# Rows of the stream's split blocks 32 bytes longer: each block at another byte modulo 256

## The chip, the cores and the metric

The kernel runs on one core of one Trainium2 chip. The metric is the device time of one execution in microseconds, as the median of the runs of a kernel. One further execution was taken with the hardware profiler; all rows below come from it.

## What is computed

A decoder trunk of two layers over 512 tokens of width 1024, all in float32. Each layer is two half-weighted SwiGLU blocks around a mixer: an mLSTM in the first layer, a sparse attention with shared keys and values (computed once, between the layers) in the second. Cut to what matters here:

```python
def swiglu(h, w_in, w_out):                      # w_in (1024, 5632), w_out (2816, 1024)
    a, b = jnp.split(h @ w_in, 2, axis=-1)
    return (jax.nn.silu(a) * b) @ w_out

for layer in range(2):
    h = h + 0.5 * swiglu(rmsnorm(h, ffn_norm[layer, 0]), ffn_w_in[layer, 0], ffn_w_out[layer, 0])
    hn = rmsnorm(h, mix_norm[layer])
    h = h + (mlstm_mixer(hn, ...) if layer == 0 else nsa_mixer(hn, kv, ...))
    h = h + 0.5 * swiglu(rmsnorm(h, ffn_norm[layer, 1]), ffn_w_in[layer, 1], ffn_w_out[layer, 1])
    if layer == 0:
        kv = nsa_shared_kv(h, ...)
```

## The kernel before

The stream is kept transposed, as eight blocks `h[b]` of 128 features by 512 tokens. Every product is made of split operands: an operand is written as a high part (rounded to the matmul's input type, `float32r`) and a low part (what is left), and `mm3` (line 145) adds three matmuls, high by high, high weight by low stream, low weight by high stream. In the trace a matmul's name is out<-moving,stationary, so the three are `pmm<-xhi,whi`, `pmm<-xlo,whi` and `pmm<-xhi,wlo`. Each has its own weight load of 128x128 (the rows of PEld), then streams the 512 columns of the moving block.

The weights come in by DMA, 512 KB at a time, into `wraw`; ScalarE and VectorE split them into `whi` and `wlo` (lines 124 and 125), two weights ahead of their use. The stream's blocks are split once per stage by `norm_in`: `parts(b)` scales block b by the norm's gain and writes `xhi` on ScalarE (line 187) and `xlo` on VectorE (line 188). All eight pairs stay for the whole stage. The pool `x` has eight buffers of each of the two tags, so block b of every stage is in buffer b. In the mixers the same buffers serve a second time, as `yhi`/`ylo` (line 559) and `ohi`/`olo` (line 947), the split inputs of the output projections, made by `split` (lines 152 and 153).

The stages follow each other: `ffn0`, `mlstm`, `ffn1`, `kv`, `ffn2`, `nsa`, `ffn3`. A `ffn` stage (line 256) goes in three parts of 8, 7 and 7 pairs of strips: for each pair, 2x8 `mm3` against the eight x blocks (line 289), then `gate` on VectorE and ScalarE gives `ghi`/`glo`, and eight output blocks of 7 or 8 `mm3` each against these (line 307). That is 22 pairs x 16 x 3 = 1056 matmuls on x blocks and 528 on g blocks in each of the four. The blocks go in the order k = 0 to 7 for one strip, then for the other (the first pair of a part goes strip by strip within k). In the mixers x blocks are the moving operand of the projections, or, in `project_v` and for the values of `kv`, the stationary one against moving weights.

How the buffers lie: pools are placed one after the other, and a buffer's start is rounded up to 32 bytes. In the program as built, the h blocks, `wraw`, `whi`, `wlo`, `xhi` and `xlo` all begin at 128 modulo 256 in each partition (the first `xhi` at byte 69248, then every 2048 bytes). A strip of 128 weights is 512 bytes, so every strip begins at 128 modulo 256 too. In the `ffn` stages a tile `home` of 384 bytes (line 262) stands ahead of the others, and `ghi` and `glo` begin at 128 modulo 256 as well. In `mlstm` the stage's own tiles begin at 192 modulo 256, in `nsa` the large ones at 0 or at 64. In `compress` of the `kv` stage the stationary operand is a slice `Fh[:, m, :]` of 124 columns, 496 bytes, so its start moves back by 16 bytes modulo 256 with each m.

The order of the instructions on each engine is that in which the code issues them; nothing in it depends on addresses.

Of the kernel before, what the change touches and what calls it, by code (L numbers as in the profile page):

```python
# [11 lines left out]
F32R = mybir.dt.float32r  # L12
# [7 lines left out]
P = 128  # L20
T = 512
# [69 lines left out]
class Net:  # L91
# [83 lines left out]
    def norm_in(self, gcol, ssq=True, loaded=False):  # L175


        nc = self.nc
        x, acc = [], []
        if ssq:  # L180
            acc = [self.sp.tile([P, T], F32, name=f"ssq{i}", tag=f"ssq{i}") for i in range(2)]

        def parts(b):
            hi = self.xp.tile([P, T], F32R, name="xhi", tag="xhi")
            lo = self.xp.tile([P, T], F32R, name="xlo", tag="xlo")
            g = self.g[:, gcol + b:gcol + b + 1]
            nc.scalar.activation(hi, self.h[b], AF.Copy, scale=g)
            nc.vector.scalar_tensor_tensor(lo, self.h[b], g, hi.bitcast(F32), op0=ALU.mult, op1=ALU.subtract)
            x.append((hi, lo))

        def squares(b):
            t = acc[b // 4]
            if b % 4 == 0:
                nc.scalar.activation(t, self.h[b], AF.Square)
            else:
                sq = self.sp.tile([P, T], F32, name="sq", tag="sq", bufs=2)
                nc.scalar.activation(sq, self.h[b], AF.Square)  # L197
                (nc.gpsimd if b < 4 else nc.vector).tensor_tensor(t, t, sq, op=ALU.add)  # L198

        for b in range(KB):  # L200
            parts(b)
            if ssq and not loaded:
                squares(b)
        if ssq and loaded:
            for b in range(KB):
                squares(b)
        if ssq:
            nc.vector.tensor_tensor(acc[1], acc[1], acc[0], op=ALU.add)
        return x, acc[-1] if acc else None
# [102 lines left out]
    def mlstm(self):  # L312
        nc, tc = self.nc, self.tc
        TT, STT, TS = nc.vector.tensor_tensor, nc.vector.scalar_tensor_tensor, nc.vector.tensor_scalar
        with ExitStack() as ctx:
# [16 lines left out]
            def pair(name, src):  # L332

                t = mp.tile([P, T], F32R, name=name, tag="rows", bufs=2)
                nc.gpsimd.memset(t.bitcast(F32), 0.0)
                nc.scalar.activation(t[:H], src, AF.Copy)
                TT(t[32:32 + H], src, t[:H].bitcast(F32), op=ALU.subtract)
                return t
# [193 lines left out]
            def finish(half):  # L532

                d = dm[half]
                s = mp.tile([40, T], F32, name="ds", tag="tmp", bufs=3)
                nc.scalar.copy(s, d[:40])
                pt = ps_nm()[:, :160].rearrange("p (t c) -> p t c", t=NTB)
                for tb in range(NTB):
                    nc.tensor.transpose(pt[:, tb, :], s[:, tb * P:(tb + 1) * P], self.ident[:40, :40])
                dc = mp.tile([P, NTB, H], F32, name="dc", tag="dc", bufs=2)  # L540
                cf = mp.tile([P, NTB, H], F32, name="cf", tag="cf", bufs=2)
                nc.scalar.activation(dc, pt[:, :, :H], AF.Square)
                TT(dc, dc, e2, op=ALU.max)
                TS(dc, dc, EPS, None, op0=ALU.mult)
                STT(dc, pt[:, :, 32:], 1.0 / P, dc, op0=ALU.mult, op1=ALU.add)
                fl = lambda t: t.rearrange("p t h -> p (t h)")
                self.rsqrt(mp, fl(cf), fl(dc), "crt")
                pr = ps_nm()
                for tb in range(NTB):
                    nc.tensor.transpose(pr[:H, tb * P:(tb + 1) * P], cf[:, tb, :], self.ident)  # L550
                cr = pair("cr", pr[:H])
                yield
                for h in range(4 * half, 4 * half + 4):
                    pc = ps_nm()
                    self.mm(pc, pick(h), cr, True, True)
                    n = num[h]
                    STT(n, n, self.g[:, G_HEAD + h:G_HEAD + h + 1], pc, op0=ALU.mult, op1=ALU.mult)
                    (nc.vector if half else nc.gpsimd).tensor_tensor(n, n, sig[h], op=ALU.mult)
                    hi = self.xp.tile([P, T], F32R, name="yhi", tag="xhi")
                    lo = self.xp.tile([P, T], F32R, name="ylo", tag="xlo")  # L560
                    self.split(n, hi, lo)
                    y[h] = (hi, lo)
                    yield
# [33 lines left out]
            run(rest)  # L597
            sigmoids(0)
            weave(project_v(1), finish(0), 0.25)
            rest = chain(project_og(1), project_out(0))  # L600
            weave(heads(1), rest, 1.0)
            sigmoids(1)
            weave(finish(1), rest, 5)
            run(rest)
            run(project_out(1))
# [165 lines left out]
    def nsa(self):  # L771
        nc, tc = self.nc, self.tc
        TT, STT, TS = nc.vector.tensor_tensor, nc.vector.scalar_tensor_tensor, nc.vector.tensor_scalar
        with ExitStack() as ctx:
# [169 lines left out]

            def project_out(half):
                for k in range(4 * half, 4 * half + 4):
                    hi = self.xp.tile([P, T], F32R, name="ohi", tag="xhi")
                    lo = self.xp.tile([P, T], F32R, name="olo", tag="xlo")
                    self.split(o[k], hi, lo)
                    y[k] = (hi, lo)  # L950
                for m2 in range(4):
                    w = self.weight("n_out", half, m2)
                    for j in range(2):
                        ps = ps_mm()
                        for k in range(4):
                            self.mm3(ps, self.strip(w, 4 * j + k), y[4 * half + k], k == 0, k == 3)
                            yield
                        hh = self.h[2 * m2 + j]
                        TT(hh, ps, hh, op=ALU.add)
# [13 lines left out]
            def all_fronts():  # L973
                for h in range(QH):
# [16 lines left out]
                    fronted[0] = h + 1  # L991

            q0, backs, out0 = project_q(0), {}, project_out(0)

            read, started, fronted, qdone = [0, 0], [0], [0], [1]
# [24 lines left out]
            while fill.step():  # L1020
                pass
            assert fill.may is None
            run(project_out(1))

    def store(self):
# [121 lines left out]
```

## Time and profile before

| | us |
|---|---|
| median of 2 runs | 2048.72 (2048.69 to 2048.75) |
| the profiled execution | 2048.92 |
| its span, first to last instruction | 2047.1 |
| PE (matmuls) busy | 2026.3, 99% of the span |
| DVE busy | 1116.5, 55% |
| ACT busy | 816.5, 40% |

What lies around the span is 1.8 us. Matmuls are pipelined: one begins while the one before it still drains, so the busy time of one (389 ns) is longer than the step from its start to the next one's start. In a stream without waits the step is what the time is made of. The duration shown is the step plus a tail of some 162 ns that overlaps the next matmul, so that a nanosecond more in the duration is a nanosecond more in the step.

### The profile page before, as it was taken

Reading aid. Unit: us, or ns where it says so; the run is one execution under the profiler, and the core shown is the slowest. Engines: PE = TensorE matmul, PEld = TensorE weight load, DVE = VectorE, ACT = ScalarE, POOL = GpSimd, SP = SyncE. Lnnn points to the kernel's source line nnn. Section 1 sums busy time; section 2 is a strip of 40 time slices with the busy share of each in tenths; the row PEclk is TensorE's granted clock in tenths of the full one; section 3 lists DMA queues with packets and bytes.
Section 4 is the critical chain, followed back from the end, with each engine's and each line's share of the span. In section 5 each row is a group of like instructions: output and inputs, shape, how many; then the busy total and the mean of one; then the engine's idle time right before and its main releaser. Section 6 shows DMA issues by size and latency. Waiting matters only on the chain.

```text
span 2047.1 us, 24445 instructions
## 1 busy us (share of the span) xinstructions
PE 2026.3 (99%) x9468; PEld 1658.9 (81%) x9468; DVE 1116.5 (55%) x1814; ACT 816.5 (40%) x1410; POOL 166.8 (8%) x216
## 2 busy tenths in 40 slices
PE   8999999999999999999999999999999999999999
PEld 6888888788878888888888888888777788888887
DVE  6434445767865434445666444445778874434343
ACT  5313223445743222234343322224889863222231
POOL 1000000012200000000101000001444310000000
PEclk9999999999999999999999999999999999999999
DMA  4232332323123332333333323323111112332323
GB/s 161 94 101 94 94 103 86 113 80 95 64 73 103 93 102 87 102 96 97 103 106 121 117 93 91 105 88 103 51 42 47 37 62 93 94 102 88 105 94 95
DMA packets 56468, 188.12 MB, mean 92 GB/s; under 512 B 6816, under 2 KB 7456, under 8 KB 56352
## 3 DMA queue, kind: packets, MB, share of 16 engines
q1 hardware_dynamic: 55392, 184.47, 28.5%
q8 instruction: 74, 1.21, 0.2%
q0 software_dynamic: 384, 1.05, 0.2%
q10 hardware_dynamic: 576, 1.05, 0.1%
q14 instruction: 42, 0.34, 0.1%
HBM read 177.10 MB, written 2.10 MB: 88 GB/s over the span
## 4 chain that ended last, share of the span: by engine, by line
PE 91%; ACT 4%; DVE 3%; issue 1%; DMA 0%; POOL 0%; SPq 0%; ACTq 0%; DVEq 0%
PE pmm L143 81%; PE S L143 2%; PE po L143 2%; PE vps L143 1%; ACT pr L889 1%; PE pt L921 1%; PE paux L143 1%; DVE wlo L125 1%; PE pn L143 1%; ACT whi L124 1%; ACT pth L152 0%; PE dm L143 0%; PE pt L143 0%; ACT nx L886 0%; DMA wraw<-in_ffn_in 0%
## 5 line engine op out<-in xcount | busy, mean ns | idle before, releaser
L124 ACT ACTIVATE whi<-wraw 128x1024 fp32r<-128x1024 f32 (+3 forms) x399 | 360.3, 916 | 993.8 <-PE pmm L143 825.7
L143 PE MATMUL pmm<-xhi,whi 128*128 128x512 f32 x1672 | 657.9, 393 | 7.7 <-ACT whi L124 7.7
L143 PE MATMUL pmm<-xhi,wlo 128*128 128x512 f32 x1672 | 654.0, 391 | 0.3 <-DVE wlo L125 0.2
L143 PE MATMUL pmm<-xlo,whi 128*128 128x512 f32 x1672 | 653.1, 391 | 0.0
L125 DVE TENSOR_TENSOR wlo<-wraw,whi 128x1024 fp32r<-128x1024 f32 (+3 forms) x399 | 421.5, 1066 | 85.2 <-ACT whi L124 74.4
L143 PEld LDWEIGHTS pmm<-xhi,whi 128*128 128x128 f32 x1672 | 314.4, 188 | 71.0 <-ACT whi L124 9.2
L143 PEld LDWEIGHTS pmm<-xhi,wlo 128*128 128x128 f32 x1672 | 314.0, 188 | 67.9 <-DVE wlo L125 2.0
L143 PEld LDWEIGHTS pmm<-xlo,whi 128*128 128x128 f32 x1672 | 314.4, 188 | 61.8
L143 PE MATMUL pmm<-ghi,whi 128*128 128x512 f32 x704 | 274.1, 389 | 0.0
L143 PE MATMUL pmm<-ghi,wlo 128*128 128x512 f32 x704 | 273.9, 389 | 0.0
L143 PE MATMUL pmm<-glo,whi 128*128 128x512 f32 x704 | 273.9, 389 | 0.0
L271 DVE TENSOR_TENSOR fu<-pmm,r 128x512 f32<-128x512 f32 x88 | 60.8, 691 | 261.3 <-PE pmm L143 261.3
L309 DVE SCALAR_TENSOR_TENSOR h<-pmm,h 128x512 f32<-128x512 f32 x96 | 66.1, 691 | 240.3 <-PE pmm L143 240.3
L269 DVE TENSOR_TENSOR ft<-pmm,r 128x512 f32<-128x512 f32 x88 | 60.8, 691 | 177.6 <-PE pmm L143 177.4
L143 PEld LDWEIGHTS pmm<-ghi,wlo 128*128 128x128 f32 x704 | 132.2, 188 | 27.5
L143 PEld LDWEIGHTS pmm<-ghi,whi 128*128 128x128 f32 x704 | 132.2, 188 | 27.3
L143 PEld LDWEIGHTS pmm<-glo,whi 128*128 128x128 f32 x704 | 132.2, 188 | 27.3
L198 POOL TENSOR_TENSOR ssq<-ssq,sq 128x512 f32<-128x512 f32 x18 | 28.8, 1600 | 1029.1 <-ACT sq L197 996.9
L894 POOL TENSOR_SCALAR pr<-pr,rz,gate 128x512 f32<-128x512 f32 (+3 forms) x128 | 82.5, 650 | 108.8 <-DVE rz L890 93.5
L152 ACT ACTIVATE ghi<-ft 128x512 fp32r<-128x512 f32 x88 | 55.7, 633 | 76.4 <-DVE ft L272 76.4
L889 ACT ACTIVATE pr<-S,nx,c 128x512 f32<-128x512 f32 (+3 forms) x128 | 78.0, 615 | 6.7 <-PE pt L921 5.6
L153 DVE TENSOR_TENSOR glo<-ft,ghi 128x512 fp32r<-128x512 f32 x88 | 60.4, 687 | 15.5 <-ACT ghi L152 15.5
(302 smaller groups left out, 2019.9 us busy)
## 6 DMA issues: line engine op xcount, KB each, us to landing
wraw<-in_ffn_in SPq DMA_DIRECT2D x176, 512.0 KB, 3.5
wraw<-in_ffn_out SPq DMA_DIRECT2D x64, 448.0 KB, 3.4
wraw<-in_ffn_out SPq DMA_DIRECT2D x32, 512.0 KB, 3.6
wraw<-in_m_qk SPq DMA_DIRECT2D x8, 512.0 KB, 3.5
wraw<-in_m_v SPq DMA_DIRECT2D x8, 512.0 KB, 3.5
wraw<-in_m_og SPq DMA_DIRECT2D x8, 512.0 KB, 3.4
wraw<-in_m_out SPq DMA_DIRECT2D x8, 512.0 KB, 3.4
wraw<-in_kv_t SPq DMA_DIRECT2D x8, 512.0 KB, 3.5
```

The source lines that it names most:

```text
L124: nc.scalar.activation(hi[:p, c], raw[:p, c], AF.Copy)
L125: nc.vector.tensor_tensor(lo[:p, c], raw[:p, c], hi[:p, c].bitcast(F32), op=ALU.subtract)
L143: self.nc.tensor.matmul(out, lhsT, rhs, start=start, stop=stop)
L152: self.nc.scalar.activation(hi, src, AF.Copy)
L153: self.nc.vector.tensor_tensor(lo, src, hi.bitcast(F32), op=ALU.subtract)
L198: (nc.gpsimd if b < 4 else nc.vector).tensor_tensor(t, t, sq, op=ALU.add)
L269: nc.vector.tensor_tensor(t, pa, r, op=ALU.mult)
L271: nc.vector.tensor_tensor(u, pb, r, op=ALU.mult)
L309: nc.vector.scalar_tensor_tensor(h, po[j], 0.5, h, op0=ALU.mult, op1=ALU.add)
L889: nc.scalar.activation(s, S[:, i, :n], AF.Exp, bias=nx[:, i:i + 1], scale=cc, accum_out=z[:, i:i + 1])
L894: nc.gpsimd.tensor_scalar(s, s, rz[:, i:i + 1], gate[:, tb, gi:gi + 1], op0=ALU.mult, op1=ALU.mult)
L921: nc.tensor.transpose(pt[:, col:col + P], pr[br][:, ROW[tb] + sb * P:ROW[tb] + sb * P + P], self.ident)
```

## The change

The buffers of the pool `x` get 520 columns in place of 512: 2080 bytes in a row, of which 512 columns are used. The high parts use columns 0 to 511; the low parts of `norm_in` use columns 4 to 515, the others 0 to 511. In the program as built, the first `xhi` still begins at byte 69248, and block b begins 32 b bytes further modulo 256: at 128, 160, 192, 224, 0, 32, 64, 96. The `xlo` of block b begins 16 bytes beyond that: at 144, 176, 208, 240, 16, 48, 80, 112. What is allocated after the pool moves up by 512 bytes, so that it keeps its place modulo 256 and modulo 512. The names of the stream's parts get a letter for the block (`xhia` to `xhih`). Every engine has the same instructions in the same order, with the same waits; only the addresses of the x, y and o blocks and of what lies behind them are others.

```diff
@@ norm_in
         def parts(b):
-            hi = self.xp.tile([P, T], F32R, name="xhi", tag="xhi")
-            lo = self.xp.tile([P, T], F32R, name="xlo", tag="xlo")
+
+            hi = self.xp.tile([P, T + 8], F32R, name=f"xhi{chr(97 + b)}", tag="xhi")[:, :T]
+            lo = self.xp.tile([P, T + 8], F32R, name=f"xlo{chr(97 + b)}", tag="xlo")[:, 4:T + 4]
             g = self.g[:, gcol + b:gcol + b + 1]
@@ mlstm, finish
-                    hi = self.xp.tile([P, T], F32R, name="yhi", tag="xhi")
-                    lo = self.xp.tile([P, T], F32R, name="ylo", tag="xlo")
+                    hi = self.xp.tile([P, T + 8], F32R, name="yhi", tag="xhi")[:, :T]
+                    lo = self.xp.tile([P, T + 8], F32R, name="ylo", tag="xlo")[:, :T]
@@ nsa, project_out
-                    hi = self.xp.tile([P, T], F32R, name="ohi", tag="xhi")
-                    lo = self.xp.tile([P, T], F32R, name="olo", tag="xlo")
+                    hi = self.xp.tile([P, T + 8], F32R, name="ohi", tag="xhi")[:, :T]
+                    lo = self.xp.tile([P, T + 8], F32R, name="olo", tag="xlo")[:, :T]
```

## Rows read from the trace of the kernel before

**Rows 1.** The page's head: span, busy time by engine (share of the span, instructions), the granted TensorE clock in 40 slices (9 is 90% or more), and the shares of the chain that ended last.
```profile
span 2047.1 us, 24445 instructions
PE 2026.3 (99%) x9468; PEld 1658.9 (81%) x9468; DVE 1116.5 (55%) x1814; ACT 816.5 (40%) x1410; POOL 166.8 (8%) x216
...
PEclk9999999999999999999999999999999999999999
...
PE 91%; ACT 4%; DVE 3%; issue 1%; DMA 0%; POOL 0%; SPq 0%; ACTq 0%; DVEq 0%
```

**Rows 2.** Busy time of PE in one stretch of each `ffn` stage: the stretch and its length, PE's busy time and number of matmuls, granted clock, share of the DMA engines, GB/s.
```profile
30.00:371.00 341.00, 341.00 (x1506) 1.00 0.30 95
622.00:969.00 347.00, 347.00 (x1532) 1.00 0.31 97
1155.00:1420.00 265.00, 265.00 (x1171) 1.00 0.31 98
1702.00:2040.00 338.00, 338.00 (x1492) 1.00 0.31 97
```

**Rows 3.** The page's groups of the matmuls on x blocks over the whole span, and one of the three on g blocks: count, busy time, mean ns of one, idle time before and what ended it.
```profile
L143 PE MATMUL pmm<-xhi,whi 128*128 128x512 f32 x1672 | 657.9, 393 | 7.7 <-ACT whi L124 7.7
L143 PE MATMUL pmm<-xhi,wlo 128*128 128x512 f32 x1672 | 654.0, 391 | 0.3 <-DVE wlo L125 0.2
L143 PE MATMUL pmm<-xlo,whi 128*128 128x512 f32 x1672 | 653.1, 391 | 0.0
...
L143 PE MATMUL pmm<-ghi,whi 128*128 128x512 f32 x704 | 274.1, 389 | 0.0
```

**Rows 4.** PE's instructions in order of time from 1061.7 to 1064.0 us, in `kv`'s left-over work between matmuls of `ffn2`: start us, duration us.
```profile
1061.74 0.39 PE L143 MATMUL pmm<-xhi,whi 128*128 128x512 f32 x1
...
1063.78 0.39 PE L143 MATMUL pmm<-xhi,whi 128*128 128x512 f32 x1
```

**Rows 5.** The same from there to 1066.3 us: matmuls.
```profile
1064.23 0.40 PE L143 MATMUL pmm<-xhi,wlo 128*128 128x512 f32 x1
1064.47 0.28 PE L143 MATMUL paux<-whi,Fh 128*124 128x256 f32 x1
1064.58 0.28 PE L143 MATMUL paux<-wlo,Fh 128*124 128x256 f32 x1
1064.70 0.28 PE L143 MATMUL paux<-whi,Fl 128*124 128x256 f32 x1
1064.82 0.40 PE L143 MATMUL pmm<-xhi,whi 128*128 128x512 f32 x1
1065.05 0.40 PE L143 MATMUL pmm<-xlo,whi 128*128 128x512 f32 x1
1065.29 0.40 PE L143 MATMUL pmm<-xhi,wlo 128*128 128x512 f32 x1
1065.52 0.39 PE L143 MATMUL pmm<-xhi,whi 128*128 128x512 f32 x1
1065.75 0.39 PE L143 MATMUL pmm<-xlo,whi 128*128 128x512 f32 x1
1065.98 0.40 PE L143 MATMUL pmm<-xhi,wlo 128*128 128x512 f32 x1
1066.21 0.28 PE L143 MATMUL paux<-whi,Fh 128*124 128x256 f32 x1
```

**Rows 6.** The weight loads of the same moments (PEld): start us, duration us.
```profile
1064.01 0.19 PEld L143 LDWEIGHTS pmm<-xhi,wlo 128*128 128x128 f32 x1
1064.23 0.18 PEld L143 LDWEIGHTS paux<-whi,Fh 128*124 128x124 f32 x1
```

**Rows 7.** PE's instructions from 1117.1 to 1119.8 us, behind another such group of three.
```profile
1117.15 0.28 PE L143 MATMUL paux<-whi,Fl 128*124 128x256 f32 x1
1117.27 0.40 PE L143 MATMUL pmm<-xhi,whi 128*128 128x512 f32 x1
1117.51 0.40 PE L143 MATMUL pmm<-xlo,whi 128*128 128x512 f32 x1
1117.74 0.39 PE L143 MATMUL pmm<-xhi,wlo 128*128 128x512 f32 x1
1117.97 0.40 PE L143 MATMUL pmm<-xhi,whi 128*128 128x512 f32 x1
1118.20 0.39 PE L143 MATMUL pmm<-xlo,whi 128*128 128x512 f32 x1
1118.43 0.39 PE L143 MATMUL pmm<-xhi,wlo 128*128 128x512 f32 x1
...
1119.79 0.39 PE L143 MATMUL pmm<-xhi,wlo 128*128 128x512 f32 x1
```

**Rows 8.** The matmuls and weight loads of line 143 between 1064 and 1150 us: count, duration in ns least/median/most, first and last start, form.
```profile
L143 PE MATMUL pmm<-xlo,whi x99: 387/389/397, 1064.0 to 1142.6; 128*128 128x512 f32 x99
L143 PEld LDWEIGHTS pmm<-xhi,wlo x99: 187/188/188, 1064.0 to 1142.6; 128*128 128x128 f32 x99
L143 PE MATMUL pmm<-xhi,wlo x99: 389/391/398, 1064.2 to 1142.8; 128*128 128x512 f32 x99
...
L143 PEld LDWEIGHTS paux<-whi,Fh x24: 183/184/185, 1064.2 to 1140.4; 128*124 128x124 f32 x24
```

**Rows 9.** Groups of matmuls on x blocks from 1064.2 to 1150 us: count, busy time, mean ns of one.
```profile
L143 PE MATMUL pmm<-xhi,wlo 128*128 128x512 f32 x99 | 38.8, 392 | 0.0
L143 PE MATMUL pmm<-xlo,whi 128*128 128x512 f32 x99 | 38.7, 391 | 0.0
L143 PE MATMUL pmm<-xhi,whi 128*128 128x512 f32 x98 | 38.6, 394 | 0.0
```

**Rows 10.** The instructions that write the x blocks in all seven stages: count, duration in ns least/median/most, first and last start, form.
```profile
L187 ACT ACTIVATE xhi<-h,gains x56: 704/710/727, 4.0 to 1683.6; 128x512 fp32r<-128x512 f32 x56
L188 DVE SCALAR_TENSOR_TENSOR xlo<-h,gains,xhi x56: 739/747/1847, 4.7 to 1685.3; 128x512 fp32r<-128x512 f32 x56
```

## The prediction

> **What bounds the kernel now.** I read the page's head first, then PE's busy time by stretch, then single matmuls in order of time. PE is busy for 2026.3 of 2047.1 us, the chain that ended last is 91% PE, and the granted clock is at its upper level, 2.4 GHz, in every slice [rows 1]. In the stretches of the four ffn stages PE has no idle time at all: 1291 us in all hold 5701 matmuls [rows 2]. One or two of each stretch's count are only cut by its edges, so the step from one start to the next is 1291 / (5701 - 7) = 226.7 ns. There nothing else can end last: the 55% of DVE and the 40% of ACT [rows 1] are hidden. A change that moves no instruction can move the time there only through this step of 226.7 ns, and a matmul that is longer by 1 ns lengthens the whole by 1 ns.
>
> So the question is what sets the step, and whether the byte at which the moving block begins has a part in it. The steady duration is 389 ns, as the mean on g blocks [rows 3] and as the median on x blocks in a mixed stretch [rows 8]. It isn't the only one. Before 1064 us nine steps are 226.7 ns each: (1063.78 - 1061.74) / 9 [rows 4]. Then, at 1064.23, a matmul of the same form takes 0.40 in place of 0.39 us, and its step is 0.24 us [rows 5]. What differs is not this matmul: it is the weight load that runs beside it. At 1064.01 that was `wlo`, which begins at 128 modulo 256 as the moving x block does; at 1064.23 it is `Fh`, which begins elsewhere (124 columns, in rows that step by 496 bytes) [rows 6]. After the three short matmuls the next five have all their operands at 128 modulo 256 again, and yet take 1065.98 - 1064.82 = 1.16 us, 232 ns each [rows 5]. A later group shows the way back: five steps of 0.24, 0.23, 0.23, 0.23 and 0.23 us, and from 1118.43 on 0.227 for good, (1119.79 - 1118.43) / 6 [rows 7]. I read this as follows: the moving stream and the weight load that runs beside it hinder each other's reads; how much depends on how they stand to each other; in a uniform stream, where every pair stands alike, the two slip within some six matmuls into the one rhythm of 226.7 ns that repeats itself, and whatever is of another length or begins at another byte throws them out of it.
>
> A rule of the Trainium skill speaks against this reading, and so against any effect. The page "SBUF — State Buffer", section "Who interferes with whom", gives TensorE two read ports of its own, one for the moving operand and one for weight loads, independent of each other, and says that TensorE never waits on anyone there. By that rule the sum below is zero; that is the first rival. This trace agrees with it only in the uniform stretches and not in [rows 5].
>
> **The change part by part.** It adds no instruction, no wait and no DMA, and moves none past another. Three things remain.
>
> *The matmuls on x blocks.* Before, the moving block and every weight strip begin at 128 modulo 256, so each pair stands alike. After, the strips still do, but the block's start takes 16 different places, and from one matmul to the next it changes: block k high, low, high, then block k+1. The uniform stream is gone in all x stretches. How many matmuls this touches: three groups of 1672 [rows 3], to which come, by the code, 288 matmuls with x as the stationary operand and 24 of the gates: 5328. Of these 4 x 1056 = 4224 are in ffn stages and now run at 226.7 [rows 2]. Of the other 1104 most are in mixed stretches. In the one of rows 8 and 9 the mean is (392 + 391 + 394) / 3 = 392.3 ns, so 3.6 over the usual 388.7 (226.7 + 162), against 5.3 in the disturbed run: some 30% still sit in the rhythm, and I take 330 of the 1104 for the rest too. That is about 4550 matmuls that have something to lose.
>
> What one loses isn't shown, as no moving block of 512 columns begins off a multiple of 64 bytes. The bounds come from the nearest rows. Below: the shortest duration of such a matmul is 387 [rows 8], a gain of 1.7 ns. Above: the longest without an outlier is 398 [rows 8], a loss of 9.3 ns. Between these stand the mean of a stretch in which disturbed and steady matmuls alternate, +3.6 [rows 9], and the run in which all are disturbed, +5.3 [rows 5]. A stream whose pairs change at each step is nearer to the second, but some of its pairs will stand well, as some in the mixed stretch do. I take +4.0 ns: 4550 x 4.0 = 18.2 us. The ends are 4550 x -1.7 = -7.7 us and 4550 x 9.3 = +42.3 us.
>
> *The matmuls on g blocks.* Their addresses stand to the weights as before, since all behind the pool moves by 512 bytes. Coming out of a disturbed x stretch each of the 12 g stretches needs some six matmuls at +5.3 ns to get back [rows 7]: 12 x 6 x 5.3 = 0.4 us. The y and o blocks come in at mixed places already and add nothing that I can size.
>
> *The writes.* 56 pairs write x blocks, 710 ns on ACT and 747 ns on DVE [rows 10]; they are on the path only at a stage's head. A start at a multiple of 16 bytes is not shown for a written block. The nearest row is a read: `Fh` loads start at all multiples of 16, and take 184 ns for 124 columns, where 188 ns are for 128 [rows 8], 1.48 and 1.47 ns a column, so no difference. I take zero. From the spread of the ACT row, 704 to 727, even 17 ns on each of the 56 writes would be 1.0 us.
>
> Sum: +18.6 us. Against the profiled execution (2048.9: the span of 2047.1 and 1.8 around it) that gives 2067.5; that execution is 0.2 us above the median of the runs, so I predict 2067.
>
> **The rivals.**
>
> *Nothing happens (2049).* What throws the stream out of its rhythm may be the short matmuls in between and not the address; a stream of 512-column matmuls alone would then settle whatever the bytes are. For it: within rows 5 the disturbed five have the same addresses as the steady ones, so address alone isn't the cause, and the return in rows 7 is quick. Against: the first slow matmul, at 1064.23, comes before any short one; only the weight load beside it is another. The time would be 2048.7 with a few tenths either way.
>
> *Slower by over 2% (2091).* The place is the x part of the ffn stages; the mechanism is the same, but with places that change at every step no pair ever stands well, and each costs what the longest costs: 398 in place of 388.7, so 42.3 us and 2091. A block that begins off a multiple of 64 bytes might also cost something of its own, for which there is no row. It decides from a mean of 398 ns on. For it: nothing lets the pairs settle, which is what ended the bad run in rows 7. Against: even in the disturbed run two of the five are at 0.39 us [rows 5].
>
> *Faster.* Some place of the block may be better than the one that the rhythm has found. From rows: if all x matmuls took 387 [rows 8], 4550 x 1.7 = 7.7 us less, 2041. To be faster by over 2% (below 2007.8) the step would have to fall by 41 / 4550 = 9 ns, to 217.7, and no row shows a 512-column matmul below 387 - 162 = 225. The Trainium skill has a rule by which there is more room: "TensorE: Matmul & The Clock Gate", section "Back-to-back issue gap", puts the step of a lone stream at N/2.4 + 2.5 ns, 215.8 for 512 columns. If the difference to the 226.7 of this trace were all a conflict that other bytes avoid, the estimate by that page is 4550 x 10.9 = 50 us less, 1999. No run here shows it.
>
> **How the numbers follow.** A change under 2% (below 2007.8 or above 2089.7 would be beyond it) is about what a measurement of this kernel tells from none. Forecast, 2055 to 2085: 0.52. Nothing happens, 2045 to 2055: 0.22. Slower by over 2%, or close to it: 0.20, of which 0.17 lies beyond the bound. Faster: 0.06, of which 0.03 beyond the bound. So faster 0.03, same 0.80, slower 0.17. The range runs from 2041, where all x matmuls are at their shortest, to 2094, the upper end of 42.3 us with 2 or 3 us for what has no row; I leave out some 0.04 below and 0.12 above.
>
> **What would show it.** In the profile after, the three x groups of the ffn stages should have a mean near 393 in place of 389, by block letter different from each other; the g groups should stay at 389 but for the first few of each stretch; PE should still be at 99% with the idle times as they are; ACT and DVE should be unchanged. If the x groups stay at 389 for every letter, the bytes play no part and the first rival holds. If they are at 398 for all, it is the second; if some letters are below 387, the third. The prediction would be wrong in its mechanism if the x groups kept 389 and the time moved all the same, through waits at a stage's head.

## The result, and the profile after

| | before | after |
|---|---|---|
| median, us | 2048.72 | 2074.97 (2074.49 to 2075.44, 2 runs) |
| span of the profiled execution, us | 2047.1 | 2073.7 |
| ratio of the times | | 1.0129, 95% interval 1.0112 to 1.0145 |

The changed kernel is 26.3 us slower. The forecast was 2067 with 2041 to 2094 as its range: the direction held, the place held, and the change stayed under 2%; the size had been put at 18.3 us (2067 less 2048.7).

The head of the page after: span, and busy time by engine, against [rows 1].
```profile
span 2073.7 us, 24445 instructions
...
PE 2053.5 (99%) x9468; PEld 1660.1 (80%) x9468; DVE 1117.0 (54%) x1814; ACT 817.0 (39%) x1410; POOL 166.0 (8%) x216
```
PE is busy for 27.2 us more with the same 9468 matmuls; DVE, ACT and POOL have moved by less than 1 us. So the time is in the matmuls and in nothing around them.

A stretch of `ffn0`, against the first of [rows 2]: stretch, length, PE's busy time and number of matmuls, granted clock.
```profile
30.00:371.00 341.00, 341.00 (x1482) 1.00 0.29 94
```
1482 matmuls where there were 1506, still without idle time and at the same clock. Where they are slower the groups of `ffn1` show, 640 to 970 us: count, busy time, mean ns of one. Before:
```profile
L143 PE MATMUL pmm<-xlo,whi 128*128 128x512 f32 x309 | 120.2, 389 | 0.0
L143 PE MATMUL pmm<-xhi,wlo 128*128 128x512 f32 x309 | 120.2, 389 | 0.0
L143 PE MATMUL pmm<-xhi,whi 128*128 128x512 f32 x308 | 119.8, 389 | 0.0
```
After:
```profile
L143 PE MATMUL pmm<-ghi,whi 128*128 128x512 f32 x165 | 64.3, 389 | 0.0
...
L143 PE MATMUL pmm<-xhih,wlo 128*128 128x512 f32 x40 | 15.9, 398 | 0.0
L143 PE MATMUL pmm<-xhih,whi 128*128 128x512 f32 x40 | 15.9, 397 | 0.0
...
L143 PE MATMUL pmm<-xhif,wlo 128*128 128x512 f32 x39 | 15.5, 398 | 0.0
...
L143 PE MATMUL pmm<-xhia,whi 128*128 128x512 f32 x39 | 15.3, 393 | 0.0
...
L143 PE MATMUL pmm<-xhia,wlo 128*128 128x512 f32 x39 | 15.2, 391 | 0.0
...
L143 PE MATMUL pmm<-xloa,whi 128*128 128x512 f32 x39 | 15.1, 388 | 0.0
```
The g groups stay at the 389 ns of [rows 3]; the x groups, all at 389 in this stage before, lie between 388 and 398 by block. The block is not all: `xhia`, which begins where it did, at 128 modulo 256 like the strips, has risen to 393 and 391, while its `xloa`, 16 bytes off, is at 388.

PE in order of time at the end of an x stretch (start us, duration us), against the steady [rows 4] and the return in [rows 7]:
```profile
701.18 0.40 PE L143 MATMUL pmm<-xhih,whi 128*128 128x512 f32 x1
...
701.88 0.39 PE L143 MATMUL pmm<-ghi,whi 128*128 128x512 f32 x1
702.12 0.39 PE L143 MATMUL pmm<-glo,whi 128*128 128x512 f32 x1
...
703.97 0.39 PE L143 MATMUL pmm<-ghi,whi 128*128 128x512 f32 x1
```
The first nine g steps still take (703.97 - 701.88) / 9 = 232 ns each, though every g block and every strip begins at 128: the way back into the rhythm takes some matmuls.

The writes of the first block, against [rows 10]: count, duration in ns least/median/most.
```profile
L188 ACT ACTIVATE xhia<-h,gains x7: 704/710/726, 4.1 to 1685.1; 128x512 fp32r<-128x512 f32 x7
L189 DVE SCALAR_TENSOR_TENSOR xloa<-h,gains,xhia x7: 743/747/752, 4.8 to 1685.8; 128x512 fp32r<-128x512 f32 x7
```
Medians of 710 and 747 ns, as before; `xloa` begins 16 bytes further. Over all 56 writes of each kind the medians are 712 and 746 ns.

From the starts of all PE instructions in both traces, the step from each to the next added up by what moves:

| step after a matmul on | count | before, us | after, us | difference |
|---|---|---|---|---|
| x blocks, moving (`pmm`) | 5016 | 1159.0 | 1183.3 | +24.3 |
| x blocks, stationary | 288 | 66.4 | 67.6 | +1.2 |
| y and o blocks | 384 | 93.2 | 94.2 | +1.0 |
| g blocks | 2111 | 478.7 | 479.3 | +0.5 |
| all else | 1668 | 238.7 | 238.3 | -0.4 |

That is +26.6, the difference of the spans. In the steady stretches of the ffn stages the mean step on x blocks went from 226.67 to 232.30 ns, +5.63. Over all 4224 x matmuls of these stages the steps add up to 22.9 us more; at the head of `ffn2` 194 of them were off the rhythm (a step below 226 or from 228 ns on) before the change already, and had less to lose.

### The profile page after: what moved, and what is told of

It reads as the page before. It is cut to its first block, busy times and chain, and to the rows that moved or that the text cites. A ratio compares the mean times of both kernels' runs of the same rounds, so it can differ in the third digit from the quotient of the medians.

```text
span 2073.7 us, 24445 instructions
## 1 busy us (share of the span) xinstructions
PE 2053.5 (99%) x9468; PEld 1660.1 (80%) x9468; DVE 1117.0 (54%) x1814; ACT 817.0 (39%) x1410; POOL 166.0 (8%) x216
## 4 chain that ended last, share of the span: by engine, by line
PE 92%; ACT 3%; DVE 3%; issue 1%; DMA 0%; POOL 0%; SPq 0%; ACTq 0%; DVEq 0%
PE pmm L143 82%; PE S L143 2%; PE vps L143 2%; PE po L143 2%; ACT pr L890 1%; PE pt L922 1%; PE paux L143 1%; DVE wlo L125 1%; PE pn L143 1%; ACT whi L124 1%; ACT pth L152 0%; PE dm L143 0%; PE pt L143 0%; ACT nx L887 0%; DMA wraw<-in_ffn_in 0%
## 5 line engine op out<-in xcount | busy, mean ns | idle before, releaser
L143 PE MATMUL pmm<-xhia,whi 128*128 128x512 f32 x209 | 84.8, 406 | 8.0 <-ACT whi L124 8.0
L143 PE MATMUL pmm<-xhib,whi 128*128 128x512 f32 x209 | 83.7, 400 | 0.0
L143 PE MATMUL pmm<-xhic,whi 128*128 128x512 f32 x209 | 83.7, 400 | 0.0
L143 PE MATMUL pmm<-xhib,wlo 128*128 128x512 f32 x209 | 83.5, 400 | 0.0
L143 PE MATMUL pmm<-xloc,whi 128*128 128x512 f32 x209 | 83.5, 399 | 0.0
L143 PE MATMUL pmm<-xhih,whi 128*128 128x512 f32 x209 | 83.3, 398 | 0.0
L143 PE MATMUL pmm<-xhif,whi 128*128 128x512 f32 x209 | 83.2, 398 | 0.0
L143 PE MATMUL pmm<-xhif,wlo 128*128 128x512 f32 x209 | 83.1, 398 | 0.0
```

Of the source, the lines that this page charges most:

```text
L143: self.nc.tensor.matmul(out, lhsT, rhs, start=start, stop=stop)
```

## The experiments

The question left by the first run was what in the addresses costs. Three theories: **A**, the change of place from one matmul to the next throws the stream out of its rhythm of 226.7 ns, and a uniform stream finds it wherever it begins; **B**, each distance, modulo 256, between the moving block's start and the weight strips' has a price of its own; **C**, a block that begins off a multiple of 64 bytes costs by itself.

To set any distance, the rows of the x pool were lengthened by 256 bytes, so that all blocks begin alike, and the columns used were shifted. Room for it came from mlstm's `sig` tiles. The cut below leaves out the y and o blocks, whose rows are lengthened alike and which are not shifted.

```diff
@@ norm_in
+            ho, lo_ = HI(b), LO(b)
-            hi = self.xp.tile([P, T], F32R, name="xhi", tag="xhi")
-            lo = self.xp.tile([P, T], F32R, name="xlo", tag="xlo")
+            hi = self.xp.tile([P, T + 64], F32R, name="xhi", tag="xhi")[:, ho:T + ho]
+            lo = self.xp.tile([P, T + 64], F32R, name="xlo", tag="xlo")[:, lo_:T + lo_]
@@ mlstm, project_og
-                    s = mp.tile([P, T], F32, name="sig", tag="sig", bufs=8)
+                    s = mp.tile([P, T], F32, name="sig", tag="sig", bufs=6)
```

The "step" below is the mean from start to start over the x matmuls in the steady stretches of the ffn stages, worked out from the trace of each run; steps over 250 ns are left out as waits. In [rows 2] it is 226.7. Line 143 of the kernel before is line 147 in the runs with longer rows.

**Longer rows, same place (`pad_all128`).** Both shifts 0.

> Rows of the x blocks 256 bytes longer, every block of the stream still at 128 modulo 256 as the weight strips are (to make room, mlstm's sig tiles have six buffers in place of eight, here and in all runs that lengthen rows by 256 bytes). This is the reference for those runs. If only the place modulo 256 matters, 2049 (2047 to 2053) with x groups at 389 ns in the ffn stages. If something else of longer rows costs (rows apart, what lies behind moved by 4096 bytes), up to 2075 as in the changed kernel.

Measured 2048.56 us, ratio 0.9997 (0.9985 to 1.0008), step 226.67. Longer rows, the smaller `sig` pool and all that moved by 4096 bytes cost nothing that can be told. The blocks now begin at two places modulo 512, and that costs nothing either. What follows is due to the place.

**All x blocks 16 bytes on (`all144`).** `ho = lo_ = 4`, in columns of four bytes.

> All x blocks, high and low, at 144 modulo 256: off the weight strips by 16 bytes, but every matmul like the next. Theory A (what costs is the change of place from one matmul to the next, a uniform stream finds its rhythm of 226.7 ns wherever it begins): 2049 to 2052, x groups 389 in the ffn stages. Theory B (each distance between moving block and weight strip has its own price): x groups anywhere from 387 to 398 and steady, 2040 to 2090. Theory C (a start off a multiple of 64 bytes costs by itself): x groups 394 or more, 2072 or more.

Measured 2070.38 us, ratio 1.0104 (1.0075 to 1.0133), step 231.66 in each of the four stages. The groups of `ffn1`, 640 to 970 us:
```profile
L147 PE MATMUL pmm<-xlo,whi 128*128 128x512 f32 x308 | 121.4, 394 | 0.0
...
L147 PE MATMUL pmm<-xhi,whi 128*128 128x512 f32 x308 | 121.4, 394 | 0.0
L147 PE MATMUL pmm<-ghi,wlo 128*128 128x512 f32 x171 | 66.6, 389 | 0.0
```
The stream is as uniform as before, every matmul stands like the next, and in the mean it never gets back to 389. Theory A, with which I had explained [rows 5 to 7], falls: the distance itself costs, for the whole of a stage.

**Only the low parts 16 bytes on (`low144`).** `ho = 0`, `lo_ = 4`.

> High parts at 128, low parts of x at 144 modulo 256, alike for all blocks: the stream repeats after three matmuls. Theory A: the place changes at two of three steps, so nearly the cost of the change, 2065 to 2075. Theory B: the price of a repeated pattern, 2045 to 2075, and the low parts differ from the high ones. Theory C: only the low parts cost, a third of all144's loss.

Measured 2071.79 us, ratio 1.0111 (1.0082 to 1.0140), step 231.99. One matmul of three is moved, and all three are slow, 640 to 970 us:
```profile
L147 PE MATMUL pmm<-xhi,wlo 128*128 128x512 f32 x310 | 122.6, 396 | 0.0
L147 PE MATMUL pmm<-xlo,whi 128*128 128x512 f32 x310 | 122.1, 394 | 0.0
L147 PE MATMUL pmm<-xhi,whi 128*128 128x512 f32 x309 | 121.5, 393 | 0.0
```
Were the prices of the matmuls independent of their neighbours, two at 226.67 and one at 231.66 would give 228.3. So theory A holds in part after all: here the high parts, at distance 0, lose its low price because a neighbour stands elsewhere.

**Blocks in steps of 32, high and low alike (`step32`).** `ho = lo_ = 8 * b % 64`, the change without its 16 bytes.

> Block b at 128 + 32 b modulo 256, high and low parts at the same place: the change without its 16 bytes. Theory A: a change of place at one step of three, about 2062 to 2070. Theory B: the mean price over eight distances, with differences by letter that stay the same from stage to stage, 2055 to 2080. Theory C: only the four blocks off a multiple of 64 cost, half of all144's loss.

Measured 2073.64 us, ratio 1.0120 (1.0091 to 1.0149), step 232.46, within 0.2 of the changed kernel's. The 16 bytes are not needed for the loss. Block a stands at distance 0 in all three of its matmuls here, and is slow too, 640 to 970 us:
```profile
L147 PE MATMUL pmm<-xhia,wlo 128*128 128x512 f32 x39 | 15.3, 393 | 0.0
...
L147 PE MATMUL pmm<-xhia,whi 128*128 128x512 f32 x38 | 15.1, 397 | 0.0
L147 PE MATMUL pmm<-xloa,whi 128*128 128x512 f32 x38 | 14.9, 392 | 0.0
```
Over the four stages its mean step is 231.1 ns, where a stream that stands at 0 throughout takes 226.67.

**Three more uniform distances (`all160`, `all192`, `all0`).** `ho = lo_` = 8, 16 and 32 columns.

> All x blocks at 160 modulo 256, 32 bytes off the weight strips, alike for all. Theory B (each distance between moving block and strip has its own price): another steady mean than all144's 231.7 ns a step, anywhere from 226 to 236, so 2045 to 2092. Theory C (a start off a multiple of 64 bytes costs, wherever the strips are): as all144, 2068 to 2073. Theory A has fallen with all144.

> All x blocks at 192 modulo 256, 64 bytes off the strips. Theory B: a price of its own, 226 to 236 ns a step, 2045 to 2092. Theory C: a multiple of 64, so no loss, 2049 with x groups at 389.

> All x blocks at 0 modulo 256, 128 bytes off the strips. Theory B: a price of its own, 2045 to 2092. Theory C: no loss, 2049.

Measured 2078.15 us (ratio 1.0144, 1.0114 to 1.0173), 2059.88 (1.0055, 1.0032 to 1.0078) and 2076.26 (1.0134, 1.0105 to 1.0164); steps 233.34, 228.94 and 233.05. At 64 bytes off the strips the stream is the second cheapest of all, but its three matmuls differ; `all192`, 640 to 970 us:
```profile
L147 PE MATMUL pmm<-xhi,whi 128*128 128x512 f32 x307 | 120.5, 392 | 0.0
L147 PE MATMUL pmm<-xhi,wlo 128*128 128x512 f32 x306 | 120.1, 393 | 0.0
L147 PE MATMUL pmm<-xlo,whi 128*128 128x512 f32 x307 | 119.5, 389 | 0.0
```
At 128 bytes off, a multiple of 64 as well, the loss is nearly that of 32 bytes. That speaks against C as the whole story; the next run takes it alone.

**Weights and x blocks moved together (`xw160`).** Rows of 2048 bytes; a pad ahead of the weights moves `wraw`, `whi`, `wlo` and the x blocks by 32 bytes, one behind the x blocks makes up the 256.

```diff
@@ setup
+        nc.vector.memset(self.wp.tile([P, 8], F32, name="wpad", tag="wpad", bufs=1)[:, :1], 0.0)
@@ norm_in, once, after the first pair
+                nc.vector.memset(self.xp.tile([P, 56], F32, name="xpad", tag="xpad", bufs=1)[:, :1], 0.0)
```

> Rows of 2048 bytes again. A pad of 32 bytes ahead of the weights and one of 224 behind the x blocks: weights and x blocks both at 160 modulo 256, g blocks and everything behind where they were. Theory B: x groups at 389 in the ffn stages, as the distance is 0 again, and the g groups, now 32 bytes off the strips, at a price of their own; 2045 to 2068. Theory C: x groups at 394 or more and g groups at 389, 2068 or more.

Measured 2062.01 us, ratio 1.0070 (1.0047 to 1.0093). 640 to 970 us:
```profile
L143 PE MATMUL pmm<-xhi,wlo 128*128 128x512 f32 x306 | 119.1, 389 | 0.0
...
L143 PE MATMUL pmm<-xlo,whi 128*128 128x512 f32 x305 | 118.7, 389 | 0.0
L143 PE MATMUL pmm<-ghi,whi 128*128 128x512 f32 x176 | 69.6, 396 | 0.0
L143 PE MATMUL pmm<-glo,whi 128*128 128x512 f32 x175 | 69.2, 396 | 0.0
```
This settles it between B and C. The x blocks, now at 160 and off a multiple of 64, are back at 389 (step 226.72), since the strips went with them. The g blocks, which nobody moved, go to 396 (step 233.34), since the strips went away from them. By the steps that is 2112 x 6.67 = 14.1 us; the time rose by 13.4. So it is not the place of either operand that has the price, but how the two stand to each other. That the distance alone decides is shown for 0, which costs the same with the strips at 128 and at 160; at each other distance the strips stood at one place only.

**The other distances (`scan1` to `scan3`).** One distance for each ffn stage, alike for its blocks, 0 in the mixers; here `scan1`:

```diff
+HI = lambda b: {0: 12, 8: 20, 16: 24, 24: 28}.get(b, 0)
+LO = lambda b: {0: 12, 8: 20, 16: 24, 24: 28}.get(b, 0)
@@ norm_in
+            ho, lo_ = HI(gcol), LO(gcol)
```

> One distance of x blocks from the weight strips for each ffn stage, alike for all its blocks: 48, 80, 96 and 112 bytes in ffn0 to ffn3, 0 in the mixers. 1056 x matmuls a stage. Theory B with equal prices (any distance but 0 costs some 5 to 6.6 ns a step): all four stages at 394 to 396 ns, 2070 to 2077. Theory B with free prices: each stage its own mean, 387 to 398. If the changed kernel's loss is the mean of the prices and the change from one matmul to the next adds nothing, the mean over all sixteen multiples of 16 is 232.3 ns a step; if changing adds, it is lower.

> The same with distances of 144, 160, 176 and 192 bytes in ffn0 to ffn3. Equal prices: 394 to 396 ns in all, 2070 to 2077. Free prices: the stages differ, 2045 to 2085.

> The same with distances of 208, 240, 4 and 8 bytes in ffn0 to ffn3. 4 and 8 bytes stay within the 16 bytes in which the strip begins. Equal prices: the first two at 394 to 396 ns. If places are told apart by 16 bytes only, ffn2 and ffn3 stay at 389, and a stage with a block begun in the middle of 16 bytes loses at most what one more 16 bytes of reading takes; if single bytes count, they too get prices of their own.

Measured, one run each: 2069.89, 2073.82 and 2080.37 us, beside 2047.89 for the kernel before. The steps of all runs with a uniform distance (x blocks, but 224 from the g blocks of `xw160`, which stand 32 bytes behind the strips):

| distance, bytes | 0 | 4 | 8 | 16 | 32 | 48 | 64 | 80 | 96 |
|---|---|---|---|---|---|---|---|---|---|
| step, ns | 226.67 | 236.66 | 233.35 | 231.66 | 233.34 | 232.38 | 228.94 | 231.11 | 233.38 |

| distance, bytes | 112 | 128 | 144 | 160 | 176 | 192 | 208 | 224 | 240 |
|---|---|---|---|---|---|---|---|---|---|
| step, ns | 231.08 | 233.05 | 233.33 | 234.28 | 231.10 | 233.33 | 234.66 | 233.34 | 234.27 |

Where one distance was run in four stages, `all144`, `all160` and `all192` agree within 0.02 ns from stage to stage; in `all0` three stages lie within 0.03 ns, and `ffn2` is 0.26 above them. The scans have each distance in one stage of one run, so differences of 0.3 ns should not be read; the larger ones stand: free prices, with 0 the cheapest, 64 next, and all others between 231.1 and 236.7. Four bytes off are the worst, so places inside 16 bytes are told apart. The dearest and the cheapest row of the scans are the three x groups of `scan3`'s `ffn2` (1200 to 1430 us) and one of `scan1`'s `ffn3` (1735 to 2060 us):
```profile
L147 PE MATMUL pmm<-xhi,wlo 128*128 128x512 f32 x224 | 89.3, 399 | 0.0
L147 PE MATMUL pmm<-xhi,whi 128*128 128x512 f32 x224 | 89.3, 399 | 0.0
L147 PE MATMUL pmm<-xlo,whi 128*128 128x512 f32 x224 | 89.3, 399 | 0.0
```
```profile
L147 PE MATMUL pmm<-xhi,wlo 128*128 128x512 f32 x302 | 117.0, 387 | 0.0
```
In the second, at 112 bytes, one matmul of three is cheaper than any group at distance 0, but its neighbours are at 398 and 392, and the three together are dearer.

In the changed kernel the high parts stand at 0, 32, ... 224 bytes and the low ones at 16, 48, ... 240. By the tables the mean is 232.04 for the first and 232.45 for the second; two high and one low to each strip pair give 232.18. Measured: 232.30. For `step32` the table gives 232.04, measured 232.46. So in the mean the change from one matmul to the next adds 0.1 to 0.4 ns to what the distances cost. Block by block the table does not hold. Worked out from the traces, over a block's three matmuls in all four stages, the mean step of block c of the changed kernel is 233.4 ns (229.7 by the table) and of block d 229.6 (232.6 by the table); in `step32` blocks a and b, at 0 and 32 bytes, take 231.1 and 231.0 (226.7 and 233.3). Where neighbours stand at different distances, the price of a matmul is not that of its own distance, and why the means come out so close is not shown.

**Everything at 128 (`all128`).** If distance is what counts, the mixers, whose own tiles begin at 192, 0 or 64, should gain from being put at 128.

```diff
@@ setup, ahead of and behind the constants
+        nc.vector.memset(c.tile([P, 24], F32, name="cpad")[:, :1], 0.0)
+        nc.vector.memset(c.tile([P, 40], F32, name="dpad")[:, :1], 0.0)
@@ ffn
-            nc.vector.memset(gp.tile([P, 96], F32, name="home", tag="home", bufs=1)[:, :1], 0.0)
+            nc.vector.memset(gp.tile([P, 96 if i < 2 else 64], F32, name="home", tag="home", bufs=1)[:, :1], 0.0)
@@ mlstm
+            nc.vector.memset(mp.tile([P, 48], F32, name="mpad", tag="mpad")[:, :1], 0.0)
@@ the shared keys and values
+        nc.vector.memset(kvp.tile([P, 32], F32, name="kpad", tag="kpad")[:, :1], 0.0)
@@ nsa, for b == 0 alone
+                    nc.vector.memset(mp.tile([P, 48], F32, name="npad", tag="npad")[:, :1], 0.0)
```

> The kernel before with pads of 96 and 160 bytes ahead of and behind the constants, 192 in mlstm, 128 in the shared keys and values and 192 in nsa (home of ffn2 and ffn3 is 256 bytes, so that g stays): moving and stationary operands of nearly all matmuls begin at 128 modulo 256 (left out: Fh, Fl, hh, hl, the constants' own stationary columns). The ffn stages should stay at 226.7 ns a step. In the mixers some 980 matmuls of 512 columns were off the rhythm before, at 232.4 ns a step in the mean. Theory B, distance alone: up to 980 x 5.7 ns = 5.6 us less, 2043 to 2046. Rival: short matmuls throw the stream out of the rhythm whatever their place, and the mixers are full of them: 2047.5 to 2049.5, no difference that can be told.

Measured 2047.81 us, ratio 0.9993 (0.9984 to 1.0002): not told from no change. The matmuls of 128x128 by 512 columns that are off the rhythm (a step below 226 or from 228 to 245 ns) went from 1018 to 910 over the whole trace, those with longer steps from 266 to 261; `pad_all128`, where the mixers' own tiles kept their places, has 998. Of the 910, 592 come within six matmuls after one of another form or after a wait, and 163 right ahead of one of another form. That fits the rival put down before this run: in the mixers it is mostly the matmuls of other forms in between, and the first few after a wait, that keep the stream out of the rhythm, and equal places alone don't bring it back. It isn't fully shown, since `Fh`, `Fl` and a few other operands were left at other places.

## Why the prediction was right, and where not

*What bounds the kernel.* Right: with 99% PE and no idle time in the ffn stages, longer steps on their 4224 x matmuls make up 22.9 of the 26.6 us.

*That the place of the block against the weights plays a part.* Right, and with it the first rival falls. The rows of before showed the effect on the moving matmul of a load at another place; `xw160` shows that what counts is how the two stand to each other, and not the place of one. The distance between what the two read is worth up to 10 ns a matmul (226.67 against 236.66). The Trainium skill's page "SBUF — State Buffer", section "Who interferes with whom", calls TensorE's two read ports independent. As far as the time of a matmul goes, these runs don't bear that out.

*That a uniform stream always finds its rhythm of 226.7 ns.* Wrong. `all144` is uniform and stays at 231.66. The rhythm belongs to distance 0, and I had only seen uniform streams at distance 0 in the trace of before. The prediction put the loss on the change of place from one matmul to the next; by the table nearly all of it, 232.18 of 232.30 in the mean, is what the distances cost without any change. The forecast held because the change also took the blocks away from distance 0. That its bounds, read from a stream disturbed by other things, were of the right size is partly luck.

*The count, 4550.* Good enough, though not all of the 4224 in the ffn stages were in the rhythm before (the head of `ffn2` was not), and the x matmuls of the mixers lost 2.6 us (24.3 + 1.2 - 22.9), where 330 x 4.0 was 1.3.

*The price, +4.0 ns.* This is the term that was mis-sized. I took a value below the disturbed run's +5.3 [rows 5], with the reason that some pairs would stand well. Measured +5.63 in the steady stretches. Some do stand well: the steps behind `xloa`, `xlob` and `xlod` average 226.2 to 226.3 ns. Others reach 236.7 (`xlof`, `xhih`), and as uniform streams only 64 of the other fifteen distances is within 2.3 ns of distance 0. The 22.9 us of the ffn stages against 4224 x 4.0 = 16.9 are 6.0 of the missing 8.0 (26.6 less 18.6); the mixers' x blocks are 1.3 more. The disturbed run of five matmuls was the better guide.

*The g blocks, 0.4 us.* Measured 0.5. *The writes, nothing.* Over all 56 the medians went from 710 to 712 and from 747 to 746 ns, so nothing that counts. What I could not size, the y and o blocks, lost 1.0 us, which is also part of what was missing.

*The rival on the slow side* put every matmul at 398 ns. A whole stage at 399 exists, at 4 bytes, but the sixteen distances of this change lie lower; the mean of the x groups was 394. *The rival on the fast side* found no room: no distance is below 226.67. The Trainium skill's page "TensorE: Matmul & The Clock Gate", section "Back-to-back issue gap", gives N / 2.4 + 2.5 ns as the gap of an isolated matmul, which the prediction called a lone stream; an estimate by it is 215.8 ns for 512 columns. No run here came near it in the mean.

What stays open is the mechanism: whether and which reads meet, why 0 and then 64 bytes are best, how the prices of neighbours act on each other, and whether the load that counts is the one beside the matmul, as [rows 5, 6] suggest, or its own. No run here tells these two apart, since in each the strips all have one place.

## What to carry to other kernels

In a stream of matmuls like this one, which never waits, where the moving block and the stationary one begin, against each other and modulo 256, was worth up to 4% of a step (226.67 against 236.66 ns): put all operands of such a stream at the same place, and look after it when a tile is added ahead of them. The sign is a group whose mean is a few ns above that of another group of the same shape, with no idle time before it. Matmuls of other forms in between give the same sign, as in the mixers, and there equal places gained nothing that could be told. Spreading the starts, as one would against conflicts of equal places, was the wrong way here.

## What the runs showed of the hardware that I had not expected

A uniform stream of 128x128 by 512-column float32r matmuls, each with its own weight load, has a steady step that depends on the distance of its operands, from 226.67 ns at 0 to 236.66 at 4 bytes, at a granted clock of 1.00. In `all144`, `all160` and `all192` it repeats to 0.02 ns from stage to stage, in `all0` to 0.3. The price is not one of each matmul: with one of three moved by 16 bytes (`low144`) all three rise, from 389 to 393, 394 and 396 ns, and in `step32` the one block that stayed at distance 0 takes 231.1 ns a step.
